# Cutting the first tile of a streaming gelu-multiply kernel into two and six rows in place of four and four

## The chip, the cores and the metric

The kernel runs on one core of a Trainium2 chip. The metric is the device time of one execution in microseconds (us), median over several runs. All runs quoted are in the fast state, granted clock 1.00. Two kernels are compared by the mean time of one's fast runs over that of the other's from the same rounds on the same chip, so a ratio is not quite that of the medians beside it. The intervals are 95%.

## The reference, cut to what matters

```
x: (32, 512, 2048) float32
x1, x2 = x[..., :1024], x[..., 1024:]
out = 0.5 * x1 * (1 + erf(x1 / sqrt(2))) * x2      # (32, 512, 1024) float32
```

134.22 MB come in and 67.11 MB go out; each element is used once.

## The kernel before

The 16,384 rows are taken as 16 tiles of 128 partitions x 8 rows. There are two x buffers and two o buffers. Loads are issued by ScalarE's queue, stores by SyncE's queue. The first tile is loaded in two pieces of four rows, computed in pieces of 2, 2 and 4 rows, and stored in two halves; the last tile is loaded whole, and computed and stored like the first.

```
    def load(i):
        ...
        for rows in (slice(0, 4), slice(4, 8)) if i == 0 else (slice(0, 8),):
            dma = nc.scalar.dma_start(out=x_tile[:, rows, :], in_=x_t[i][:, rows, :])
    ...
    load(0)
    load(1)
    for i in range(n_tiles):
        ...
        pieces = i == 0 or last
        steps = ((0, 2), (2, 4), (4, 8)) if pieces else ((0, 8),)
        for lo, hi in steps:
            rows = slice(lo, hi)
            gelu = ... nc.scalar.activation(out=x_tile[:, rows, :half], in_=..., func=GELU)
            mul = nc.vector.tensor_mul(out=o_tile[:, rows, :], in0=..., in1=...)
            ...
            if pieces and hi % 4 == 0:
                part = slice(hi - 4, hi)
                nc.sync.dma_start(out=o_t[i][:, part, :], in_=o_tile[:, part, :])
        if not pieces:
            nc.sync.dma_start(out=o_t[i], in_=o_tile)
        ...
        if i + 2 < n_tiles:
            load(i + 2)
```

Load i+2 goes into the buffer of tile i, so it is issued when the mul of tile i is done. The mul of tile i+2 writes the o buffer of tile i, so it waits until the store of tile i has landed.

## Time and profile before

| | before |
|---|---|
| time, median | 470.66 us (470.19 to 470.92, 6 runs) |
| span of the profiled run | 468.8 us |
| VectorE / ScalarE busy | 139.5 us (30%) / 114.2 us (24%) |
| DMAs | 17 loads, 18 stores |
| gelu of the last tile starts | 448.55 us |
| last data packet ends | 467.57 us |

How to read it: the engines have time to spare, while the row of DMA shares stands at nine tenths to the end. So the place to look is the DMA engines. The lines are shown in the prediction.

One correction belongs here. The times of single packets in the prediction (1.99, 24.65, 457.73, 458.09, 467.81 us and the like) were read against an origin 0.24 us later than the one of the timeline, so each reads 0.24 us too late beside an instruction's time. From here on, packet times are in the timeline's own clock: the last tile's stores begin at 457.49 in the kernel before, and the last packet ends at 467.57. In one clock the slack that the prediction puts at 2.7 us is 2.47 us (store issued at 455.02, first packet at 457.49).

### The profile page before, as it was taken

How to read it: one execution, taken by the hardware profiler on the slowest of the kernel's cores; microseconds unless marked ns; L12 is line 12 of the kernel's file. 1: busy time of each engine (PE TensorE's matmuls, PEld its weight loads, DVE VectorE, ACT ScalarE, POOL GpSimd, SP SyncE). 2: the span in 40 equal slices, each digit the busy share in tenths (PEclk: the TensorE clock that was granted, in tenths of full speed). 3: DMA queues.
4: the chain of work that ended last, by engine and by line, in shares of the span. 5: the costliest groups of instructions: out<-in, count | busy, mean ns of one | idle time of the engine just before them, and what ended most of it. 6: DMA issues, size and time to landing. Idle time of an engine off the chain costs nothing.

```text
span 468.8 us, 150 instructions
## 1 busy us (share of the span) xinstructions
DVE 139.5 (30%) x20; ACT 114.2 (24%) x21; POOL 0.2 (0%) x4
## 2 busy tenths in 40 slices
DVE  0330333407033070430704207052070510606142
ACT  1320505041050410505005050140501405023060
POOL 0000000000000000000000000000000000000000
DMA  8999999999999999999999999999999999999998
GB/s 358 447 447 447 414 389 495 403 403 447 481 414 403 447 403 492 403 433 417 492 403 403 447 492 403 403 447 447 447 403 439 411 492 403 403 447 492 403 403 358
DMA packets 5041, 201.33 MB, mean 429 GB/s; under 512 B 561, under 2 KB 561, under 8 KB 561
## 3 DMA queue, kind: packets, MB, share of 16 engines
q10 hardware_dynamic: 2448, 134.22, 66.3%
q1 hardware_dynamic: 2592, 67.11, 33.2%
q14 instruction: 1, 0.00, 0.0%
HBM read 134.22 MB, written 67.11 MB: 429 GB/s over the span
## 4 chain that ended last, share of the span: by engine, by line
DMA 72%; DVE 14%; ACT 12%; ACTq 1%; issue 0%
DMA x_tile<-in_x_dram 72%; DVE o_tile L77 14%; ACT x_tile L72 12%; ACTq L119 0%; ACTq L58 0%
## 5 line engine op out<-in xcount | busy, mean ns | idle before, releaser
L77 DVE TENSOR_TENSOR o_tile<-x_tile 128x8192 f32<-128x8192 f32 (+2 forms) x20 | 139.5, 6985 | 320.7 <-ACT x_tile L72 320.7
L72 ACT ACTIVATE x_tile<-x_tile 128x8192 f32<-128x8192 f32 (+2 forms) x20 | 113.0, 5662 | 339.4 <-DMA x_tile<-in_x_dram 339.4
L72 ACT ACT_TABLE_LOAD x1 | 1.3, 1283 | 2.1 <-issue 2.1
L108 POOL MEMSET const-bfloat16-1.0<- 128x1 bf16 x1 | 0.1, 102 | 0.0
L108 POOL MEMSET const-uint8-127<- 128x1 uint8 x1 | 0.1, 102 | 0.0
L108 POOL MEMSET const-float32-0.0<- 128x1 f32 x1 | 0.1, 99 | 0.2 <-issue 0.2
L108 POOL MEMSET const-float32-1.0<- 128x1 f32 x1 | 0.1, 99 | 0.0
## 6 DMA issues: line engine op xcount, KB each, us to landing
out_dram<-o_tile SPq DMA_DIRECT2D x14, 4096.0 KB, 42.4
x_tile<-in_x_dram ACTq DMA_DIRECT2D x2, 4096.0 KB, 16.8
out_dram<-o_tile SPq DMA_DIRECT2D x4, 2048.0 KB, 18.0
x_tile<-in_x_dram ACTq DMA_DIRECT2D x15, 42.2
```

The source lines that it names most:

```text
L72: nc.scalar.activation(out=x_tile[:, rows, :half], in_=x_tile[:, rows, :half], func=GELU)
L77: mul = nc.vector.tensor_mul(out=o_tile[:, rows, :], in0=x_tile[:, rows, :half], in1=x_tile[:, rows, half:],)
L108: nc = _bacc.Bacc("TRN2", target_bir_lowering=False, num_devices=1)
```

## The change

The intent: a first piece of two rows lands sooner, so that compute and the first store begin sooner; the remaining six rows follow as one piece.

```
-        for rows in (slice(0, 4), slice(4, 8)) if i == 0 else (slice(0, 8),):
+        for rows in (slice(0, 2), slice(2, 8)) if i == 0 else (slice(0, 8),):
...
-        steps = ((0, 2), (2, 4), (4, 8)) if pieces else ((0, 8),)
+        steps = ((0, 2), (2, 8)) if i == 0 else ((0, 2), (2, 4), (4, 8)) if last else ((0, 8),)
...
-            if pieces and hi % 4 == 0:
-                part = slice(hi - 4, hi)
+            if i == 0 or (last and hi % 4 == 0):
+                part = slice(lo if i == 0 else hi - 4, hi)
```

## The prediction

> **What bounds the kernel now.** I read the page first: its engine rows and the two transfer rows of its 40 slices.
>
> ```profile
> DVE 139.5 (30%) x20; ACT 114.2 (24%) x21; POOL 0.2 (0%) x4
> ...
> DMA  8999999999999999999999999999999999999998
> ...
> HBM read 134.22 MB, written 67.11 MB: 429 GB/s over the span
> ```
>
> VectorE and ScalarE idle two thirds of the time; the DMA engines are at nine tenths in every slice but the first and the last. No gap is left inside. The chain of waits, read second, looks different at first sight:
>
> ```profile
> 274.43 0.02 issue
> 274.46 7.04 ACT x_tile L72
> 281.50 0.02 issue
> 281.52 8.70 DVE o_tile L77
> 290.22 0.02 issue
> 290.24 42.19 DMA x_tile<-in_x_dram
> ```
>
> It puts 26% of the span on the two engines, but it only follows one x buffer: gelu, mul, then the next load of that buffer, 42.2 us. The same pattern returns after 58.0 us (274.43 to 332.43), that is 29.0 us a tile, and a tile moves 8.39 + 4.19 = 12.58 MB: 434 GB/s. While one buffer computes, the other one's load runs. So what bounds it is the transfers' throughput: 201.33 MB / 434 GB/s = 463.9 us of the 468.8.
>
> What decides this case is how loads and stores share the engines. I asked for the transfers by queue (q10 carries loads, q1 stores) in stretches between landings, here 24.6 to 47.2 us and 71.4 to 100.4 us:
>
> ```profile
> q10 hardware_dynamic: 144, 8.39, 86.3%
> q1 hardware_dynamic: 134, 1.93, 20.0%
> ```
> ```profile
> q10 hardware_dynamic: 144, 8.39, 66.7%
> q1 hardware_dynamic: 144, 4.19, 33.6%
> ```
>
> 144 packets are one whole DMA: 128 partitions' data (8 for each of 16 engines) and 16 completions. Where both queues hold work they go **packet for packet**, whatever the packets' sizes: one load DMA of 64 KiB packets takes one store DMA along, be its packets 16 KiB (first pair) or 32 KiB (second). From the trace's records of single packets: 64 KiB 2.42 us, 32 KiB 1.21, 16 KiB 0.61. So a packet costs about 0.007 us plus its bytes at 27 GB/s, and cutting a tile otherwise costs nothing by itself.
>
> The tail, from the timeline of the last part:
>
> ```profile
> 448.55 7.22 ACT L72 ACTIVATE x_tile<-x_tile 128x2048 f32<-128x2048 f32 x3 [21.98 <-DMA x_tile<-in_x_dram]
> ...
> 455.02 5.57 SPq L87 DMA_DIRECT2D out_dram<-o_tile  x2
> 455.80 4.42 DVE L77 TENSOR_TENSOR o_tile<-x_tile 128x4096 f32<-128x4096 f32 x1 [0.81 <-ACT x_tile L72]
> ```
>
> The last load is in at 448.55; the first half of the last store is issued at 455.02, 6.47 us later, and the second at 460.26, 11.71 us later. The engines are full meanwhile only because the store of tile 14 is still in the queue: its last packets end at 458.09, and the last tile's first ones start at 457.73, by the packet records. The last packet ends at 467.81 and the span 1.0 us after. So the last store is there about 2.7 us before it is needed. **That slack is small, and the change can spend it.**
>
> [...]
>
> **The change part by part.** Instruction orders compared: one gelu and one mul fewer in the first tile, same number of DMAs (17 loads, 18 stores), same bytes, and the same 128 data packets per DMA; nothing changes after the first tile.
>
> 1. Compute: two rows, then six. The six-row gelu is 3.61 + 2048 x 0.835 ns = 5.32 us, the six-row mul 4.43 + 2048 x 1.042 ns = 6.56 us. Saved: one start of each, some 0.2 us, on idle engines: nothing on the end.
> 2. First load piece: 8 packets of 16 KiB an engine, 4.9 us in place of 9.7 us. Landing 12.88 - 4.85 = 8.0 us. Gelu 1.90, mul 2.29: the first store (1 MiB, 8 KiB packets of about 0.31 us) is issued at 12.2 in place of 19.34.
> 3. When does it get in? Before, the first store was issued at 19.34 and its first packet ran at 24.65: the turns at about 20.7 and 22.1 were already given to loads. With loads of 48 KiB packets (1.82 us each, from 7.5 us) the turns at 12.9 and 14.7 are lost likewise, and the store starts at about 16.5, while the second load piece still has three packets to go. Four of its eight packets go before that piece's completion, at 23.2. The piece is seen at about 23.6 (before: 22.57).
> 4. Second store and load 2: 23.6 + 5.32 + 6.56 = 35.5 us (before: 30.68). Load 1 has to the 44th us at least to run, so the load queue isn't empty: no hole.
> 5. Load 1 (8 packets from 23.2): four go with the rest of the first store, 4 x (2.42 + 0.31), then some alone, until the second store, issued at 35.5, gets in 4 to 5 us later: at about 41.4, one or two turns before load 1 ends (about 46 us, before 47.16).
>
> So at that point eight packets of the first store and about two of the second have gone, where before only eight of the first had. **The stores run two turns ahead of before.** From then on they go packet for packet, so nothing takes the lead away through the remaining tiles.
>
> 6. The tail. All bytes but the last tile's store are gone at about 458.1 in either case, as the engines never idle before. But two more store packets lie ahead of the last load's end: it lands 2 x 1.21 = 2.4 us later, at about 451.0. Its store follows 6.47 us later, at 457.4, and needs at least the 1.25 us that the first load took from issue (0.74) to its first packet (1.99): 458.7 at the earliest, after the queue ran dry at 458.1. Its second half: 451.0 + 11.7 + 1.25 to 2.2, then 8 packets x 0.607 = 4.9, then 1.0 to the end: 469.9 to 470.8, against 468.8. Sum: **+1.1 to +2.0 us**, I take +1.3, all of it in the last 12 us: 470.62 + 1.3 = 471.9.
>
> **The rivals.**
> (a) It is hidden: the stores gain one turn or none. The last load then lands at most 1.2 us later, the store is issued at 456.2, and the slack of 2.7 us swallows it: 470.6. For it: turns are whole packets, and my two turns come from lags I have seen once.
> (b) It pays: the first store starts 7 us sooner, so work ends sooner. Against it: the engines are never idle between 2 and 467.8 us, and bytes and packets are the same; only the 2 us at the start and the 1 us at the end aren't transfer, and neither is touched. Nothing under about 470.3 is to be had.
> (c) Load 2, issued 5 us later, starves the load queue. Against it: it comes some 10 us before load 1 is through; before there were 16.5. It would make a hole of some us at 45 us.
> (d) The lead is three turns or more, or a store from an empty queue takes over 2 us to begin: 473 to 474.
>
> **Range and chances.** Floor 470.4 from (b); two turns with 1.25 to 2.2 us give 471.7 to 472.6; (a), about one in four, gives 470.6; three turns, about one in eight, 473. So 471.9, eight in ten within 470.5 to 473.1. Two per cent is 9.4 us; nothing that I see comes near: same 0.98, faster 0.01, slower 0.01.
>
> **What would show it.** Steps 2 to 5: first gelu at 8.0, second at 23.6, tile 1's at 46; store issues at 12.2 and 35.5; no slice of the DMA row below nine in the first 50 us. Step 5's lead: in the steady part still 29.0 us a tile, but the last tile's gelu at about 451 in place of 448.55. Step 6: a stretch around 458 to 460 in which no packet moves. If the last gelu starts at 448.6 and no hole shows, (a) holds. The prediction is wrong if the lead doesn't last through the steady part[...], or if packets don't alternate one to one with 8 KiB stores beside 48 KiB loads.

A span of 469.9 to 470.8 us against 468.8 is +1.1 to +2.0 us, of which it takes +1.3, so 470.62 + 1.3 = 471.9 us. The upper end of its lag from issue to first packet, 2.2 us, and the "over 2 us" of rival (d) were guesses, and no trace shows them; 1.25 us is what the prediction read from the kernel before, and 0.83 us was measured in the changed one. The slopes of step 1 come from the kernel before: gelus of 1.90, 3.61 and 7.03 us for 2048, 4096 and 8192 elements (3.42 us for the last 4096: 0.835 ns each) and muls of 2.29, 4.43 and 8.69 us (4.27 us for the last 4096: 1.042 ns each).

## The result, and the profile after

The changed kernel takes 471.71 us (471.59 to 471.92, 6 runs) against 470.66 us: ratio 1.0023, interval 1.001 to 1.0036. That counts as the same at 2%, yet it is a real loss of 1.05 us: the slowest run before is faster than the fastest one after.

The page of the changed kernel, the rows that answer to those of before:

```profile
DVE 139.5 (30%) x19; ACT 114.1 (24%) x20; POOL 0.2 (0%) x4
...
DMA  9999999999999998999999999999999999999998
...
HBM read 134.22 MB, written 67.11 MB: 428 GB/s over the span
```

The first slice rose from eight to nine tenths and one slice near 180 us shows eight; slices of 11.7 us are too coarse to show a gap of half a microsecond. The start of its timeline:

```profile
7.95 1.91 ACT L72 ACTIVATE x_tile<-x_tile 128x2048 f32<-128x2048 f32 x1 [4.57 <-DMA x_tile<-in_x_dram]
...
12.22 24.09 SPq L87 DMA_DIRECT2D out_dram<-o_tile  x2
24.02 5.32 ACT L72 ACTIVATE x_tile<-x_tile 128x6144 f32<-128x6144 f32 x1 [14.16 <-DMA x_tile<-in_x_dram]
...
35.97 0.37 ACTq L58 DMA_DIRECT2D x_tile<-in_x_dram  x1
46.78 7.03 ACT L72 ACTIVATE x_tile<-x_tile 128x8192 f32<-128x8192 f32 x1 [17.43 <-DMA x_tile<-in_x_dram]
```

The first gelu starts 4.93 us sooner (before: 12.88), the first store is issued 7.12 us sooner (before: 19.34), and tile 1's gelu starts 0.38 us sooner (before: 47.16). So the change does what it was meant to do. The end of the timeline shows where that went:

```profile
451.02 7.22 ACT L72 ACTIVATE x_tile<-x_tile 128x2048 f32<-128x2048 f32 x3 [21.90 <-DMA x_tile<-in_x_dram]
...
457.48 5.57 SPq L87 DMA_DIRECT2D out_dram<-o_tile  x2
458.27 4.43 DVE L77 TENSOR_TENSOR o_tile<-x_tile 128x4096 f32<-128x4096 f32 x1 [0.81 <-ACT x_tile L72]
```

The last tile's gelu starts at 451.02, which is 2.47 us **later** than before. All that follows is shifted with it. In stretches of the end (the last two columns are the DMA share and GB/s; a packet counts where it starts) the kernel before has

```profile
457.90:458.30 0.40, 0.40 (x1) 0.00 (x0) 0.00 (x0) 1.00 1.24 532
458.30:463.40 5.10, 1.93 (x1) 0.00 (x0) 0.00 (x0) 1.00 0.98 421
```

and the changed kernel

```profile
457.90:458.30 0.40, 0.03 (x1) 0.33 (x1) 0.00 (x0) 1.00 0.00 0
458.30:463.40 5.10, 4.39 (x1) 0.00 (x0) 0.00 (x0) 1.00 0.97 411
```

Zero: by the packet records the store of tile 14 ends at 457.85 in both kernels, and in the changed one the first packet of the last tile's store starts only at 458.31 to 458.46, depending on the engine. A second, shorter gap follows before its second half: 463.40 to 463.55 to 463.70. The sum is 0.6 to 0.9 us of the 1.06 us by which the last packet ends later (468.63 against 467.57); the rest, some 0.2 us for each engine, is spread over single packets that took longer than others of their size.

Why the last load lands later shows in the count of transfers by queue (q10 loads, q1 stores). From the last tile's gelu to the end, the kernel before still has this to store:

```profile
q1 hardware_dynamic: 416, 7.86, 89.5%
```

and the changed one this:

```profile
q1 hardware_dynamic: 384, 6.82, 84.3%
```

That is 32 packets less, two for each of the 16 engines: each engine had moved two store packets more ahead of the last load's end. It was so from the start. Up to tile 1's gelu (47.16 us before, 46.78 us after) the store queue had moved

```profile
q1 hardware_dynamic: 144, 2.10, 10.4%
```

before, and

```profile
q1 hardware_dynamic: 192, 2.23, 11.2%
```

after: in bytes hardly more, in packets 48 more. The first store came 7.12 us sooner, so that half of its packets went beside tile 0's second load piece. By the packet records these 8 KiB packets (0.31 us each) mostly ran one between two load packets of 48 or 64 KiB, as the 16 KiB packets (0.61 us each) ran one between two of 64 KiB in the kernel before: a packet of 8 KiB took a turn as one of 16 KiB did. The 48 are counted at two starts of a gelu and with completions. Counted by the packet records at the end of tile 1's load data (46.18 us before, 45.49 after), 128 and 160 store packets with data had started; at the end of the last load's data (446.95 and 449.38) it was 1,920 and 1,952. So the lead is 32 packets, two an engine, at both ends. In between nothing changed in the amounts; a tile in the steady part (103 to 132 us in the changed kernel) is one load DMA against one store DMA, as before:

```profile
q10 hardware_dynamic: 144, 8.39, 66.7%
q1 hardware_dynamic: 144, 4.19, 33.5%
```

### The profile page after: what moved, and what is told of

Same layout as the page of the kernel before. It is cut to its first block, busy times and chain, and to the rows that moved or that the text cites. A ratio compares the mean times of both kernels' runs of the same rounds, so it can differ in the third digit from the quotient of the medians.

```text
span 469.9 us, 148 instructions
## 1 busy us (share of the span) xinstructions
DVE 139.5 (30%) x19; ACT 114.1 (24%) x20; POOL 0.2 (0%) x4
## 2 busy tenths in 40 slices
DMA packets 5040, 201.33 MB, mean 428 GB/s; under 512 B 560, under 2 KB 560, under 8 KB 560
## 4 chain that ended last, share of the span: by engine, by line
DMA 72%; DVE 14%; ACT 12%; ACTq 1%; issue 0%
DMA x_tile<-in_x_dram 72%; DVE o_tile L77 14%; ACT x_tile L72 12%; ACTq L119 0%; ACTq L58 0%
## 5 line engine op out<-in xcount | busy, mean ns | idle before, releaser
L77 DVE TENSOR_TENSOR o_tile<-x_tile 128x8192 f32<-128x8192 f32 (+3 forms) x19 | 139.5, 7344 | 323.2 <-ACT x_tile L72 323.2
L72 ACT ACTIVATE x_tile<-x_tile 128x8192 f32<-128x8192 f32 (+3 forms) x19 | 112.9, 5950 | 342.0 <-DMA x_tile<-in_x_dram 342.0
```

Source lines behind the costliest of these rows:

```text
L72: nc.scalar.activation(out=x_tile[:, rows, :half], in_=x_tile[:, rows, :half], func=GELU)
L77: mul = nc.vector.tensor_mul(out=o_tile[:, rows, :], in0=x_tile[:, rows, :half], in1=x_tile[:, rows, half:],)
```

## The experiments

The theory, called **turns**, is read from the counts above, 144 load packets to 144 store packets at 2.42 and 1.21 us each: while both queues held work, each DMA engine took one packet from the load queue and one from the store queue in turn. What the first tile's cut changes is how many store packets have gone when the load stream ends. Two turns ahead of before means two store packets (2 x 1.21 us) in front of the last load's landing; the slack at the end is smaller, so the engines run dry before the last store is issued.

The rivals: (1) the small first piece itself costs, by its packets or its early start; (2) the larger second compute piece holds back load 2; (3) for the runs with an altered tail, that tail is a gain or a loss by itself.

| run | median us | ratio to before (interval) | last tile's first gelu | empty stretch at the end |
|---|---|---|---|---|
| before | 470.66 | | 448.55 | none |
| changed kernel | 471.71 | 1.0023 (1.001 to 1.0036) | 451.02 | 457.85 to 458.31 |
| loads 2+6 only | 470.80 | 1.0005 (0.9992 to 1.0017) | 445.09 | none |
| stores 2+6 only | 471.85 | 1.0028 (1.0015 to 1.004) | 451.05 | 458.0 to 458.3 |
| changed, tail in four | 470.82 | 1.0004 (0.9991 to 1.0017) | 450.97 | none |
| before, tail in four | 470.60 | 0.9999 (0.9985 to 1.0013) | 448.51 | none |
| 1+7 throughout | 471.36 | 1.0016 (1.0002 to 1.003) | 450.44 | none |
| one store for tile 0 | 473.46 | 1.0059 (1.0046 to 1.0071) | 452.89 | 458.5 to 460.2 |
| before, last load 4+4 | 475.29 | 1.0099 (1.0085 to 1.0113) | 438.97 | 462.8 to 467.0 |
| changed, last load 4+4 | 473.09 | 1.0057 (1.0044 to 1.0069) | 438.82 | 462.7 to 464.7 |
| before, last compute 4+4 | 470.56 | 0.9993 (0.998 to 1.0007) | 448.86 | none |
| changed, last compute 4+4 | 472.91 | 1.0043 (1.003 to 1.0056) | 450.92 | 457.8 to 459.9 |
| 1+7, second store cut | 470.95 | 1.0002 (0.9989 to 1.0015) | 449.08 | none |
| 8 x 1 throughout | 473.25 | 1.0051 (1.0036 to 1.0066) | 451.14 | none |

The kernel before gave medians of 470.59 to 470.77 us beside these. Two executions stand apart: one of 11 of the kernel before, beside the last rounds, took 472.79 us, and one of five of "changed, last load 4+4" 474.24 us; why isn't known. All runs were correct.

### Which part of the change does it

Loads alone, in the kernel before:

```
-        for rows in (slice(0, 4), slice(4, 8)) if i == 0 else (slice(0, 8),):
+        for rows in (slice(0, 2), slice(2, 8)) if i == 0 else (slice(0, 8),):
```

> Loads of tile 0 in two and six rows, compute and stores as before. Theory (turns): both half stores of tile 0 now come after the second load piece, so the stores fall behind before's by about three turns; the last tile's gelu starts earlier than before's 448.55 us (about 445), no stretch without packets near 458 us, time as before, 470.7 us. Rival 1 (the small first piece, its packets or its early start cost the 1 us): time as the changed kernel's, 471.7. Rival 2 (the larger second compute piece holds back load 2): as before, 470.7, because compute is in the old pieces.

Measured 470.80 us, last gelu at 445.09, no gap. The first gelu started at 7.84 us, so the small, early first piece is there, and nothing is lost: rival 1 falls as far as the loads go.

Stores alone (the first two rows, then six, computed in the old pieces):

```
-            if pieces and hi % 4 == 0:
-                part = slice(hi - 4, hi)
+            if (i == 0 and hi != 4) or (last and hi % 4 == 0):
+                part = slice((0 if hi == 2 else 2) if i == 0 else hi - 4, hi)
```

> Loads and compute of tile 0 as before, only its two stores hold two and six rows. Theory (turns): the first store is issued about two us earlier than before (17 us), and the stores run two turns ahead as in the changed kernel; last gelu at about 451.0, hole of about half a us at 458, time 471.7 us. Rival 1 (loads' small first piece costs): 470.7. Rival 2 (larger compute piece): 470.7, as compute is in the old pieces.

Measured 471.85 us, last gelu at 451.05. The same stretches as above, for this run:

```profile
457.90:458.30 0.40, 0.01 (x1) 0.36 (x1) 0.00 (x0) 1.00 0.00 0
458.30:463.40 5.10, 4.42 (x1) 0.00 (x0) 0.00 (x0) 1.00 0.97 411
```

They can hardly be told from the changed kernel's. Its compute pieces are those of before, so rival 2 falls too. The stores' cut by itself brings the whole loss.

### Filling the gap at the end

The changed kernel, with the last tile computed and stored in four pieces of two rows:

```
-... ((0, 2), (2, 4), (4, 8)) if last else ((0, 8),)
+... ((0, 2), (2, 4), (4, 6), (6, 8)) if last else ((0, 8),)
-            if i == 0 or (last and hi % 4 == 0):
-                part = slice(lo if i == 0 else hi - 4, hi)
+            if pieces:
+                part = slice(lo, hi)
```

> The changed kernel, with the last tile computed and stored in four pieces of two rows. Theory (turns): the lead of two turns stays (last gelu at about 451.0), but the first piece of the last tile is issued 2.2 us sooner and the last store is only 1 MiB, so the hole at 458 us fills and the time goes back to 470.7. Rivals 1 and 2 (the loss is made in the first tile): 471.7 stays.

And that tail in the kernel before:

> Control: the kernel before with that same tail. Theory (turns): no hole to fill, so 470.7, within 0.2 us of before; last gelu at 448.6. If the four-piece tail is a gain by itself (rival 3): about 1 us less than before, 469.7.

Measured 470.82 and 470.60 us. With the tail in four the changed kernel's last gelu still starts at 450.97, so the lead is still there, but its stretches are now

```profile
457.90:458.30 0.40, 0.40 (x1) 0.38 (x1) 0.00 (x0) 1.00 1.11 471
458.30:463.40 5.10, 3.51 (x2) 0.00 (x0) 0.00 (x0) 1.00 1.00 424
```

full, and the loss is gone within the noise. In the kernel before, where no gap was to be filled, that tail changes nothing. A loss made in the first tile couldn't be mended at the last one; this and the pair before show that the loss is made at the end and goes with the gap.

### Spending the slack from the other side

The last tile computed in two pieces of four rows (its stores unchanged), in each kernel:

```
-... ((0, 2), (2, 4), (4, 8)) if last ...
+... ((0, 4), (4, 8)) if last ...
```

> The kernel before, the last tile computed in two pieces of four rows (stores as before), so its first store is issued about 8.1 us after the last load's landing in place of 6.47, its second 12.6 in place of 11.7. Theory (slack of the tail): the 2.7 us that the store queue still covers take this up just so: no hole or one below 0.3 us, 470.6 to 470.9 us. Rival (later last store is simply later by 0.9 to 1.6 us): 471.5 to 472.2.

> The changed kernel with the same last tile in two pieces of four rows. Theory (slack of the tail): no slack is left there, so this edit, free in the kernel before, costs its whole delay here: hole of about 2.2 us from 458.1, time about 472.7 to 472.9. Rivals 1 and 2 (a fixed cost of the first tile): 1.0 us above the same edit of before, 471.7.

Measured 470.56 and 472.91 us. The stretch from 457.9 to 459.8 us is, in the kernel before with this tail,

```profile
457.90:459.80 1.90, 1.90 (x1) 0.00 (x0) 0.00 (x0) 1.00 0.98 414
```

and in the changed one

```profile
457.90:459.80 1.90, 1.90 (x2) 0.14 (x1) 0.00 (x0) 1.00 0.00 0
```

The same delay of the last store is free in one kernel and costs about 1.2 us in the other (472.91 - 471.71, from different rounds). The slack existed before and is used up by the change.

### Turns or bytes

If the queues shared by bytes, a first half of the last load would land sooner and let the last compute start sooner at no cost. If they share by turns, a load in two DMAs takes 16 turns (tile 0's load in two DMAs was 16 data packets an engine in the kernel before, the other loads 8), and 16 store packets go along with it.

```
-        for rows in (slice(0, 4), slice(4, 8)) if i == 0 else (slice(0, 8),):
+        for rows in (slice(0, 4), slice(4, 8)) if i in (0, n_tiles - 1) else (slice(0, 8),):
```

> The kernel before with its last load cut into two halves of four rows (32 KiB packets). Theory (turns): the last tile's load now takes 16 turns an engine and lets 16 store turns pass, so no store is left when it ends; its second half's gelu, mul and store lie bare: hole of 4 to 5 us at about 463, time about 475.3 us. Rival (shares by bytes[...]): first gelu of the last tile some 10 us earlier and time the same or up to 1 us less, 469.7 to 470.7.

The same cut of the last load in the changed kernel:

> The changed kernel with its last load cut into two halves. Theory (turns): the store queue runs empty as in the same cut of before, but its two turns of lead now mean that the loads end sooner relative to it: hole 2.3 to 3.5 us, time 472.9 to 474.1, that is below the same cut of the kernel before by 1 to 2.4 us: the sign of the change turns round. Rivals 1 and 2 (a fixed cost of the first tile): above the same cut of before by 1 us.

Measured 475.29 and 473.09 us. In the kernel before with this cut the last tile's first gelu starts 9.6 us sooner (438.97) and the time is 4.7 us longer, because its second piece starts at 458.11 with no store left to run beside it:

```profile
462.90:464.60 1.70, 1.70 (x1) 0.00 (x0) 0.00 (x0) 1.00 0.00 0
464.60:467.00 2.40, 1.59 (x1) 0.00 (x0) 0.00 (x0) 1.00 0.00 0
```

In the changed kernel the same stretches are

```profile
462.90:464.60 1.70, 0.93 (x1) 0.00 (x0) 0.00 (x0) 1.00 0.00 0
464.60:467.00 2.40, 0.00 (x0) 0.00 (x0) 0.00 (x0) 1.00 1.04 437
```

The sign of the change turns round: here it is 2.2 us faster. No fixed cost of the first tile can do that. By its packet records the store queue, two turns ahead, moved nothing from about 436 to 442 us; loads went alone meanwhile, and the second piece starts at 455.76. Here, where no store is left to hide that piece behind, the sooner load wins by 2.2 us.

### Further along the same line

One 4 MiB store for tile 0 in place of two of 2 MiB, all else as before:

```
-            if pieces and hi % 4 == 0:
+            if last and hi % 4 == 0:
...
-        if not pieces:
+        if not last:
```

> Loads and compute of tile 0 as before, but one 4 MiB store in place of two of 2 MiB. Theory (turns): eight store turns fewer stand in the queue, so stores get ahead of loads and then just keep up with compute: last gelu at about 451 us, hole at 458, 471.8 us (472 to 473 if the first store misses one more turn). A rival that counts bytes, packets or DMA overhead: one DMA less, larger packets, 470.6 or less.

Measured 473.46 us: fewer, larger DMAs, and the greatest loss of the cuts to tile 0. By the count of DMAs eight store turns are missing (one DMA fewer, at 8 data packets an engine as in the kernel before), the last gelu starts at 452.89, and from 458.53 to 460.18 us no packet starts. The result lies 0.5 us above the upper end of what was expected. The packet records say where that is: the load packets just before the store queue first came into use, at 34 us, took 1.01 us longer than others of their size. I had not reckoned with that.

Pieces of one and seven rows:

```
-... (slice(0, 2), slice(2, 8)) if i == 0 ...          -... ((0, 2), (2, 8)) if i == 0 ...
+... (slice(0, 1), slice(1, 8)) if i == 0 ...          +... ((0, 1), (1, 8)) if i == 0 ...
```

> The change taken further: tile 0 loaded, computed and stored in pieces of one and seven rows. Theory (turns): all but one or two of the first store's turns are spent beside the second load piece, and the second store comes later (38 us), too late for load 1; counted turn by turn the lead is one, not two: last gelu near 449.8, the 2.7 us of slack covers it, no hole, 470.7 us. Rival 1 (the smaller the first piece the dearer): at least 471.7, about 472.

Measured 471.36 us, between the two expectations: **a miss for the theory as it stood.** It was right on the end (no empty stretch at 458 us), but 0.8 us are lost all the same. They are lost at 40 us: the load packets that ran just before the store queue came back, after a pause, took 1.20 us longer per engine than their like; in the kernel before the corresponding excess, at 22 us, is 0.24 us. Part is given back by a start that costs 0.35 us less (0.26 against 0.61 us of excess in the first packets). To see what that excess depends on, the seven rows' store was cut into three and four rows:

```
+                parts = ((1, 4), (4, 8)) if i == 0 and lo else ((lo, hi),) if i == 0 else ((hi - 4, hi),)
+                for a, b in parts:
+                    nc.sync.dma_start(out=o_t[i][:, a:b, :], in_=o_tile[:, a:b, :])
```

> The one and seven row kernel again, which lost 0.8 us without a hole at the end: there the load packets at 40 us, just before the store queue came back, took 1.2 us longer than others of their size. Here the second store is cut into three and four rows (12 and 16 KiB packets). If the long packets go with the size of the first store packets after a pause: excess at 40 us falls to about 0.3 us as in the kernel before (16 KiB packets: 0.24), time 470.7. If they go with the pause of the store queue (15 us): excess stays at 1.2 us, time 471.4. In both the stores run eight turns less ahead: last gelu near 440 to 441 us, no hole at the end.

Measured 470.95 us, with an excess of 0.62 us at 40 us and another 0.30 us at 64 us. It lies between the two expectations and decides neither: with store packets of 12 KiB the excess at 40 us was smaller than with those of 28 KiB (0.62 against 1.20 us), but not 0.3 us. What makes these packets long stays open. And the last gelu started at 449.08, not at 440: another miss, with the same cause as the next one.

Eight pieces of one row each:

```
+... tuple(slice(k, k + 1) for k in range(8)) if i == 0 ...      # loads
+... tuple((k, k + 1) for k in range(8)) if i == 0 ...           # steps and stores
```

> Tile 0 loaded, computed and stored in eight pieces of one row: smallest pieces, earliest first store (7.7 us), 14 DMAs more than the kernel before. Theory (turns): 64 store turns for tile 0 in place of 16, so stores fall behind loads, 16 packets left when the last load ends, last gelu near 439 us, no hole; only the small cost of more packets: 470.8 to 471.2. Rival 1 (small first pieces or an early first store cost time): clearly above the changed kernel's 471.7.

Measured 473.25 us, last gelu at 451.14: **a miss**, and by the numbers alone it would speak for rival 1. The turns are as expected at first. Between 30 and 88 us the two queues moved

```profile
q10 hardware_dynamic: 392, 23.59, 93.9%
q1 hardware_dynamic: 390, 1.41, 5.9%
```

nearly the same number of packets, some 17 times the bytes for loads: the stores of one row (4 KiB packets) fall far behind. What I had left out is the o buffer. From the timeline of this run:

```profile
69.18 7.03 ACT L72 ACTIVATE x_tile<-x_tile 128x8192 f32<-128x8192 f32 x1 [13.53 <-DMA x_tile<-in_x_dram]
91.33 8.69 DVE L77 TENSOR_TENSOR o_tile<-x_tile 128x8192 f32<-128x8192 f32 x1 [26.96 <-DMA out_dram<-o_tile]
100.06 0.37 ACTq L58 DMA_DIRECT2D x_tile<-in_x_dram  x1
```

The mul of tile 2 waits 27 us for the stores of tile 0 to land. So load 4 is issued at 100.06, after the load queue had run empty at 89.2; from then to 102.8 only stores move, which takes back their lag, and between 100.48 and 100.88 nothing moves at all. Gap, long packets on restart (0.4 us and 1.36 us more of excess than before, in all) and the 96 added data packets an engine (0.7 us, an estimate from the prediction's 0.007 us a packet) make up the 2.5 us. In the run with the cut second store the same wait (28.7 us, mul at 88.74) reset the lag without an empty stretch. So in these runs the order of the queues is held between two bounds: stores too far ahead of the loads, and the tail is bare (457.85 to 458.31 us in the changed kernel); too far behind, and the mul waits for its o buffer (27.0 us here). One more detail of the expectation failed: the first store was issued at 9.27 and not at 7.7 us, as ScalarE first issued nine loads (0.73 to 5.60 us).

No version beats the kernel before clear of the noise. There data packets run without a break from 1.75 to 467.57 us of a span of 468.8 us. With the same bytes, what a cut of the tiles might still take from that is, by this trace, the excess over usual packet times: 0.61 us in the first packets and 0.24 us at 22 us. No run came out ahead by it.

## Why the prediction was right

It said 471.9 us; 471.71 us were measured. Point by point:

- **Bound by the transfers, no gain from an early start.** Right. The first store is issued 7.1 us sooner and nothing comes of it; rival (b) is out. What sets the measured 434 GB/s was not shown by any run.
- **Steps 1 and 2.** Right: six-row gelu 5.32 us, mul 6.56 us, first gelu at 7.95 (8.0 said), first store at 12.22 (12.2).
- **Step 3.** Right in kind: by the packet records the first store's packets begin at 16.34 us, beside the second load piece, and four of them go before its last data packet has been signed off. From issue that was 4.1 us (12.22 to 16.34), where the kernel before took 5.07 us (19.34 to 24.41), both with loads queued. The second gelu came at 24.02 and not 23.6. Completions are the packets of 4 bytes in the records, 16 a DMA. In the changed kernel the piece's data ended at 22.94 to 23.32 us, a store packet of 8 KiB followed on each engine, and the completions stand behind that, at 23.24 to 23.63. The last load of the kernel before shows the same: data to 446.95, a store packet to 448.16 at the latest, completions at 447.79 to 448.16, gelu at 448.55. With no store queued (its first piece, data to 12.52) the completions stand right behind the data, at 12.00 to 12.51, and the gelu started at 12.88.
- **Step 4.** Right: load 2 at 35.97 (35.5), no gap near 45 us; rival (c) is out.
- **Step 5, the lead of two turns.** Right: tile 1's gelu at 46.78 (46 said), and a lead of two packets an engine from tile 1's load (128 against 160 packets) to the last. One detail was left out: in these traces a completion, though it lasts only 0.009 us, stands where a turn of its queue would be. In the changed kernel the completions of loads and stores fall at different moments. At 66.0 us two loads run in a row where a store's completion took the store's turn, at 73.3 us two stores run in a row where a load's completion took the load's, and likewise in the next tiles (95.0 and 102.3, 124.0 and 131.3 us) and in the last (443.1 and 450.3): one turn is lost and one won back. At 66.0 us an empty store queue would look the same, as the next store had been issued only 3.5 us before; but in the run "loads 2+6 only" it happens at 107.2 us with the next store issued some 19 us before. The prediction had not looked at completions: that the two cancel was not foreseen.
- **Step 6, the tail.** Right: last gelu at 451.02 (451.0), its store issued at 457.48 (457.4), the queue dry before it. The term that was off is the lag from issue to first packet, 1.25 us said: it was 0.83 us here (457.48 to 458.31). Half of the error is the clock offset named above. Two other terms were too short by about as much: from the last packet's end to the end of the span it is 1.26 us (1.0 said, the offset again), and the second half's eight packets took 5.08 us across the engines (463.55 to 468.63; 4.9 said). So the lower end of the sum, 469.9, meets the measured span of 469.9 partly by luck. The loss is 1.05 us, where 1.3 was taken and 1.1 to 2.0 given as its range.
- **Rival (a), hidden.** Wrong for this change, but true for a neighbour: the kernel before with its last tile's store delayed stays at 470.56 us.
- **Rival (d).** Out: the lead was two turns and the lag from an empty queue 0.83 us, not over 2.

That the stores' lead and the gap cause the loss is shown: by the stores' cut alone, by the filled gap, by the slack spent from the other side, and by the change of sign. That packets alternate is shown, for the traces read here, by the counts of 144 to 144 and 392 to 390. What makes load packets long just before a paused store queue comes back (by 0.24 us in the kernel before, 0.40 us in the changed one, 1.01 us with one store, 1.20 us with one and seven rows) stays open.

## What to carry to other kernels

In this stream, bound by DMA, cut points hardly changed the sum of the transfers (the same 201.33 MB, with packets of 64 KiB at 2.42 us and of 32 KiB at 1.21 us in both kernels), but they did change the order, and with it what is left to hide the last tile's compute and store behind. Where the trace shows two queues sharing the engines packet for packet, as here (144 to 144, 392 to 390), count turns and not bytes: here store packets of 4 KiB went one for one with load packets some 17 times their size on average, and a load cut in two DMAs was 16 data packets an engine in place of 8. Cutting the last load so cost 4.7 us (475.29 against 470.59). Before cutting the first tile more finely, look at the end of the trace for the slack between the last store's issue and the moment the queue runs dry (2.47 us here), and mend the tail first: the tail in four took the changed kernel from 471.71 to 470.82 us.
